# Block 1's output projection and the choice of four of its heads, moved ahead of the attention of blocks 2 and 3

## The chip, the cores and the metric

The kernel runs on one NeuronCore of a Trainium2 chip. Its five engines work side by side, each through a queue of its own in a fixed order: TensorE (PE, matrix products; PEld is its weight load), VectorE (DVE), ScalarE (ACT), GpSimd (POOL) and SyncE (SP, which here only issues transfers). What counts is the time of one execution on the device in microseconds. All arrays are float32.

## The reference

Two layers work on 512 tokens of width 1024. Only the first is touched by the change. It puts 16 learned tokens ahead, mixes by attention and a recurrence side by side, and then sends each token through a sum over experts chosen for it:

```python
proj = jnp.einsum('btd,dc->btc', a, w_in)
att = diff_attention(aq, ak, av, ...)      # 4 heads, two softmax maps each, blocks of 128 queries
rec = hgrn2(rq, rf, ri, rg, ...)           # gated recurrence, 4 heads
h = h + jnp.einsum('btc,cd->btd', jnp.concatenate([att, rec], -1), w_out)

def one_block(xb):                         # 128 tokens
    q = jnp.einsum('nd,dc->nc', xb, w_query).reshape(128, 8, 2, 128)
    s = jnp.einsum('nhpc,hpkc->nhpk', q, subkeys)
    sv, si = lax.top_k(s, 16)
    cand_s = sv[:, :, 0, :, None] + sv[:, :, 1, None, :]
    top_s, pos = lax.top_k(cand_s.reshape(128, 8, 256), 16)
    experts, gates = ..., softmax(top_s)   # 8 heads x 16 = 128 experts per token
    hid = gelu(einsum('nkd,nd->nk', u_table[experts], xb)) * gates
    return einsum('nk,nkd->nd', hid, v_table[experts])
```

Attention of a block of tokens needs the keys and values of itself and of the blocks ahead of it, and nothing of their attention's result. The output projection of a block needs that block's attention and recurrence alone; the choice of its experts needs its projection alone.

## The kernel before

The 512 tokens lie in four blocks of 128 (0 to 3), their running sum in `h`. Each block has 128 expert slots per token, and for each slot one **gather** (`gather`, L801) fetches for all 128 tokens the row of u and the row of v that token needs: 1 MB, by an indirect DMA that POOL issues, into one of six buffers `g`. DVE multiplies it with `xb` and sums (`dot`, L815); after each pair of slots ACT takes the gelu and DVE multiplies with the gate (L860); then the v half is added to `h` either by DVE (L834) or by PE through a diagonal matrix into `acc` (L829), as the table `PE_SLOTS` says. Only then is the buffer free for another gather. There are 512 gathers, and this text calls the 128 of block b **expert stage b**.

Everything else is woven among the gathers by hand. Each part of the program is a Python generator that yields after a step; `weave(main, side, rate)` takes `rate` steps of the side for every step of the main one, and one gather is one main step (130 in a stage). A scheduler then sets the last order of each engine's queue from that, and may shift instructions by some places.

- Stage 0 runs beside `until_first()`, that is `mixer([1, 2, 3])` up to its `yield "first"`, at 0.5 steps per gather; what is left of these steps when the gathers are used up follows without gathers.
- Stage 1 runs beside the rest of that mixer at 0.62, and then beside the selection of blocks 2 and 3 from scores kept aside (`slow[0]`, a fifth of a step each).
- Stage 2 runs beside what is left of that selection (`slow[1]`, a third of a step each), stage 3 beside the second layer for blocks 0 to 2, and block 3's second layer comes last.

In `mixer([1, 2, 3])` come projections and recurrence, then the attention of its three blocks (`attend`, seven steps for four heads and two more), `project_out` (L580 on PE with weights `wout`, L587 adds to `h`), then `choose_from` (the transposed rows `xT`, the row norm `rstd`) and `choose`: per head, queries by `wq` (L171), scores into the PSUM tile `psc` (L711), and for blocks 0 and 1 at once `select`, which finds the top 16 and computes the experts' numbers `idx` and the gates on DVE (L743 to L793). For blocks 2 and 3 the scores are kept. `ALONE` is the number of heads that block 1 chooses by itself, ahead of "first"; the others are chosen for blocks 1 to 3 in one product of 384 columns, and blocks 2 and 3 make up for the first `ALONE` heads afterwards in products of 256 columns. `need(b, g)` takes steps at once where a stage comes to the gathers of heads that aren't chosen yet; four heads give 64 gathers.

PSUM tiles of the tag "tr" are two: `psc`, the transposes `awT`, `tf`, `mxT` and the attention's result `aO` take turns in them.

Of the kernel before, what the change touches and what calls it, by code (L numbers as in the profile page):

```python
# [26 lines left out]
GROUPS = ((0, 1, 16), (1, 1, 8), (2, 2, 5), (4, 4, 3), (8, 8, 1))  # L27
NCAND = sum(n * w for _, n, w in GROUPS)
PE_SLOTS = {0: (8, 8, 16, 8), 1: (20, 24, 28, 26), 2: (16, 26, 10, 24), 3: (0, 0, 0, 0)}
RATE = {"1b": 0.5, "1c": 0.62, "2a": 0.62}  # L30
GBUFS = 6
RR = (2.8, 2.7)
FR = 2.0
PRE = 0
ANCHOR = 124
ALONE = 2
PACE = (5, 3)

CW = 256
# [3 lines left out]
def layer_pair_kernel(ctx: ExitStack, tc, a, dbg=None):  # L43
# [151 lines left out]
    def run(*gens):  # L195
        for g in gens:
            for _ in g:
                pass

    def chain(*gens):  # L200
        for g in gens:
            yield from g

    def weave(main, side, per, flush=True):

        due = 0.0
        for _ in main:
            yield
            due += per
            while due >= 1.0:  # L210
                due -= 1.0
                next(side, None)
        for _ in side if flush else ():
            yield
# [223 lines left out]
    def mixer(blocks, meta):  # L438

        nb = len(blocks)  # L440
# [34 lines left out]
        def cols(i):  # L475
            return slice(off + i * P, off + (i + 1) * P)
# [29 lines left out]
        def heads_to_features(po, tag, use):  # L506
            o = head_norm(po, tag)
            p4 = psum_t("mxT").rearrange("p (k t) -> p k t", k=4)
            for k in range(4):
                T.transpose(p4[:, k, :], o[:, k, :], ident)  # L510
            use(p4)
# [14 lines left out]
        def attend(i, b):  # L526
            dst = aq[:, :, cols(i)]
            o = t1.tile([P, 4, P], F32, tag="ao", name="ao")
            yield from attention_block(b, dst, lambda hd, po: V.tensor_copy(o[:, hd, :], po))
            yield  # L530
            heads_to_features(o.rearrange("p h v -> p (h v)"), "0",
                              lambda p4: V.tensor_scalar(dst, p4, subw, None, op0=ALU.mult))
            yield
# [55 lines left out]
        def project_out(part):  # L589
            for j in range(2):  # L590
                p = [(psum, psum, psum_c)[i]("wout") for i in range(len(part))]
                for half in (1, 0):
                    yield from out_half(j, half, part, p)
                out_add(j, part, p)
# [15 lines left out]
        def values(part):  # L610
            return tokens(2, lambda i: av[:, blocks[i], :], avm, part)

        if nb > 1:
            recs = [recurrent(i, blocks[i]) for i in range(nb)]
            yield from weave(chain(kq(None), values((0, 1))), chain(*recs), RR[0])
            yield from weave(feature(6, use_g, lo=off), attend(0, blocks[0]), RR[1])
            for i in range(1, nb):
                yield from attend(i, blocks[i])
            yield from project_out(list(range(nb)))
            choice = new_choice(blocks)  # L620
            yield from choose_from(choice, blocks[:1])
            yield from choose(choice, blocks[:1], range(ALONE))
            yield "first"
            yield from choose_from(choice, blocks[1:])
            yield from choose(choice, blocks, range(ALONE, 8))
            yield from choose(choice, blocks[1:], range(ALONE))
        else:
            rec = recurrent(0, blocks[0])
            for _ in feature(6, use_g, lo=off):
                yield  # L630
                next(rec)

            def also_rec(g):
                for _ in g:
                    yield
                    next(rec, None)

            yield from also_rec(kq((0,)))
            with after(state["load"]):
                for b in range(1, NB):  # L640
                    nc.sync.dma_start(h[:, b, :], x[b * P:(b + 1) * P, :])
                load_choice()
            yield from also_rec(values((0,)))
            wh = [None, None]
            att = attend_out(blocks[0], wh)
            yield from islice(att, 3)
            yield from also_rec(kq((1,)))
            yield from islice(att, 3)
            yield from also_rec(values((1,)))
            yield from rec  # L650
            for j in range(2):
                next(att)
                p = [psum("wout")]
                w = load_out(j, 1)
                with after(state["av"]):
                    for k in range(4):
                        T.matmul(p[0], qq[:, k, cols(0)], w[:, k, :], start=(k == 0), stop=(k == 3))
                out_add(j, [0], p)
                wh[j] = load_out(j, 0)
                yield  # L660
            yield from att
# [14 lines left out]
    def choose_from(choice, blocks):  # L676
        at, xT = choice
        for b in blocks:
            to_features(h[:, b, :], P, xT[:, :, at[b]], ffw)
            V.tensor_copy(rstd[:, b:b + 1], row_rstd(h[:, b, :], P, "", new_xn()))  # L680
            yield
# [154 lines left out]
    def experts(b):  # L836


        xb = make_xb(b, rstd[:, b:b + 1], t1.tile([P, D], F32, tag="xb", name="xb"))
        pe = by_pe(b)  # L840
        before = []
        for j in range(0, P + 2, 2):
            if j == P:
                for late in before:
                    add_row(b, *late)
                    yield
                return
            need(b, j // 32)
            d2 = t2.tile([P, 2], F32, tag="dots", bufs=4, name="dots")
            h2 = t2.tile([P, 2], F32, tag="hid", bufs=4, name="hid")  # L850
            now = []
            for i in range(2):
                g = gather(b, j + i)
                dot(b, j + i, xb, g, d2[:, i:i + 1])
                now.append((j + i, pe, g, h2[:, i:i + 1]))
                if before:
                    add_row(b, *before[i])
                yield
            S.activation(h2, d2, AF.Gelu)  # L859
            V.tensor_tensor(h2, h2, gate[b].rearrange("p h k -> p (h k)")[:, j:j + 2], op=ALU.mult)  # L860
            before = now
# [391 lines left out]
    def tally(name, g):  # L1253
        for v in g:
            steps[name] = steps.get(name, 0) + 1
            yield v
# [21 lines left out]
    slow = [paced(later, k) for k in PACE]  # L1278
# [8 lines left out]

    run(weave(experts(0), weave(tally("1b", until_first()), first, FR), RATE["1b"]))
    run(weave(experts(1), chain(tally("1c", rest), tally("1d", slow[0])), RATE["1c"], flush=False))
    run(rest)  # L1290
    load_second()
    run(weave(experts(2), tally("2z", slow[1]), RATE["1c"]))
    run(weave(experts(3), tally("2a", second([0, 1, 2])), RATE["2a"]))
    run(tally("2b", second_last(3)))
    if dbg is not None:
# [84 lines left out]
```

## Time and profile before

| | us |
|---|---|
| median of 3 runs (2003.7 to 2016.32) | 2010.13 |
| the profiled execution | 2004.79 |
| its span, first to last instruction | 2003.0 |

The profile shows one execution. A busy share is the part of a stretch in which an engine executed something; the DMA share is the mean of 16 transfer engines; PEclk is the clock that TensorE was granted, as a share of full speed. A view by windows adds these up over stretches of the span. A row of waits names an instruction, what released it, and the idle time ahead of it.

### The profile page before, as it was taken

The page shows a single profiled execution, that of the slowest core. Times are in us where ns is not written, and L with a number is a line of the kernel's source. Part 1 is how long each engine was busy: PE and PEld are TensorE (multiplying, and loading weights), DVE is VectorE, ACT ScalarE, POOL GpSimd, SP SyncE. Part 2 cuts the span into 40 slices and gives each one's busy share as a digit, 9 for nine tenths or more (in the row PEclk, how much of TensorE's full clock was granted, in tenths as well). Part 3 has the DMA queues.
Part 4 walks back from the last instruction along what each step waited for, and adds up shares of the span by engine and source line. Part 5 has one row for each costly group of instructions (what it writes and reads, how often), then busy time and mean ns, then how long its engine had stood idle before and what let it go on. Part 6 is the DMA issues. An engine that isn't in the chain of part 4 may idle for free.

```text
span 2003.0 us, 18269 instructions
## 1 busy us (share of the span) xinstructions
PE 1551.6 (77%) x5391; PEld 910.2 (45%) x5391; DVE 1628.4 (81%) x3944; ACT 609.1 (30%) x1255; POOL 684.0 (34%) x523
## 2 busy tenths in 40 slices
PE   8967898988788996667665575464699976888697
PEld 7844575753345563222222122121366543547475
DVE  3589999968987899997579956867967988788887
ACT  2213311236641232211121211011147642231574
POOL 0014333323420333444443445545533344443000
PEclk9988999998788997798896686679799978999799
DMA  9439998987884998999999999999998779999664
GB/s 391 181 145 368 385 357 330 346 305 280 322 301 149 394 364 320 341 354 377 402 404 345 360 384 394 416 395 402 388 391 320 288 249 355 404 385 359 251 232 178
DMA packets 94557, 666.57 MB, mean 333 GB/s; under 512 B 10789, under 2 KB 11230, under 8 KB 14330
## 3 DMA queue, kind: packets, MB, share of 16 engines
q0 software_dynamic: 73728, 536.90, 69.5%
q1 hardware_dynamic: 19394, 123.42, 15.9%
q10 hardware_dynamic: 1336, 5.08, 0.6%
q8 instruction: 43, 0.70, 0.1%
q14 instruction: 56, 0.46, 0.1%
HBM read 663.27 MB, written 2.10 MB: 332 GB/s over the span
## 4 chain that ended last, share of the span: by engine, by line
DVE 33%; PE 28%; issue 16%; DMA 10%; POOL 8%; ACT 5%; POOLq 0%; SPq 0%; ACTq 0%; DVEq 0%
PE win L171 15%; DVE g L815 11%; POOL g L801 8%; DMA g<-in_peer_uv_dram,idx 8%; DVE h L834 6%; PE wout L171 2%; DMA win<-in_w_in_dram 1%; DVE jt L764 1%; DVE ex L767 1%; DVE jt L766 1%; ACT L859 1%; PE acc L829 1%; PE pl L1129 1%; PE pl L1130 1%; DVE si L747 1%
## 5 line engine op out<-in xcount | busy, mean ns | idle before, releaser
L801 POOL DMA_INDIRECT g<-in_peer_uv_dram,idx x512 | 680.9, 1330 | 1148.4 <-DVE h L834 435.6
L815 DVE SCALAR_TENSOR_TENSOR g<-g,xb 128x1024 f32<-128x1024 f32 x512 | 622.8, 1217 | 147.2 <-DMA g<-in_peer_uv_dram,idx 144.4
L829 PE MATMUL acc<-g,dg 128*128 128x512 f32 x856 | 511.1, 744 | 272.9 <-ACT dg L826 272.8
L829 PEld LDWEIGHTS acc<-g,dg 128*128 128x128 f32 x856 | 187.8, 233 | 559.2 <-ACT dg L826 371.7
L171 PE MATMUL win<-aT,win 128*128 128x384 f32 (+2 forms) x1344 | 366.7, 428 | 26.9 <-DMA win<-in_w_in_dram 20.1
L834 DVE SCALAR_TENSOR_TENSOR h<-g,hid,h 128x1024 f32<-128x1024 f32 x298 | 381.0, 1279 | 3.6
L171 PEld LDWEIGHTS win<-aT,win 128*128 128x128 f32 x1344 | 228.6, 196 | 150.2 <-issue 28.9
L859 ACT ACTIVATE hid<-dots 128x2 f32<-128x2 f32 x256 | 52.1, 203 | 784.0 <-DVE g L815 777.8
L171 PE MATMUL wq<-xT,wq 128*128 128x128 f32 (+2 forms) x576 | 120.5, 361 | 2.1 <-DVE qq L490 2.1
L826 ACT ACTIVATE dg<-ident,hid 128x128 f32<-128x128 f32 x214 | 80.7, 398 | 87.3 <-DVE hid L860 72.3
L859 ACT ACT_TABLE_LOAD x79 | 101.4, 1283 | 11.0 <-DVE g L815 9.7
L171 PEld LDWEIGHTS wq<-xT,wq 128*128 128x128 f32 x576 | 86.2, 193 | 31.3 <-issue 5.9
L860 DVE TENSOR_TENSOR hid<-hid,gate 128x2 f32<-128x2 f32 x256 | 40.3, 158 | 60.7 <-ACT hid L859 60.4
L171 PE MATMUL win<-win,aT 128*128 128x256 f32 x384 | 86.9, 382 | 0.0
L1125 DVE TENSOR_TENSOR wlo<-wl,whi 128x1024 fp32r<-128x1024 f32 x60 | 72.3, 1218 | 11.9 <-PE pl L1130 5.0
L171 PEld LDWEIGHTS win<-win,aT 128*128 128x128 f32 x384 | 72.2, 191 | 11.9 <-issue 1.6
L1124 ACT CAST whi<-wl 128x1024 fp32r<-128x1024 f32 x60 | 60.1, 1047 | 29.8 <-DMA wl<-in_w_in_2t_dram 12.3
L379 PE MATMUL sc<-akT,aq 64*128 64x400 f32 (+3 forms) x80 | 32.9, 511 | 19.6 <-ACT ae L389 19.6
L149 PE MATMUL tf<-ident,xn 128*128 128x128 f32 x56 | 12.2, 382 | 40.3 <-DVE xn L973 22.4
L171 PE MATMUL wout<-wout,mg 128*128 128x256 f32 x192 | 41.9, 380 | 0.1
L815 DVE DVE_READ_ACCUMULATOR g<-g,xb 128x1 f32 x512 | 41.5, 81 | 0.0
L926 DVE TENSOR_TENSOR_SCAN rs<-kp,zero 128x128 f32<-128x128 f32 (+3 forms) x32 | 26.3, 823 | 18.2 <-ACT kp L924 18.1
(386 smaller groups left out, 1869.3 us busy)
## 6 DMA issues: line engine op xcount, KB each, us to landing
win<-in_w_in_dram SPq DMA_DIRECT2D x50, 1024.0 KB, 9.1
wq<-in_peer_w_query_dram SPq DMA_DIRECT2D x18, 1024.0 KB, 8.3
wl<-in_w_in_2t_dram SPq DMA_DIRECT2D x18, 1024.0 KB, 4.8
wout<-in_w_out_dram SPq DMA_DIRECT2D x12, 1024.0 KB, 8.5
g<-in_peer_uv_dram,idx POOLq DMA_INDIRECT x512, 8.6
wl<-in_w_in_2t_dram ACTq DMA_DIRECT2D x4, 1024.0 KB, 8.8
wl<-in_w_out_2t_dram SPq DMA_DIRECT2D x4, 1024.0 KB, 4.8
skT<-in_peer_subkeys_dram SPq DMA_DIRECT2D x9, 256.0 KB, 7.7
```

What stands on the lines that cost most here:

```text
L171: T.matmul(o, lhs(k), rhs(k), start=(k == 0), stop=(k == nk - 1))
L379: T.matmul(sc[:, 0:hi - lo], aq[rr, hd, :], akT[rr, hd, lo:hi], start=True, stop=(hi != L))
L801: G.indirect_dma_start(out=g, out_offset=None, in_=uv_tab, in_offset=bass.IndirectOffsetOnAxis(ap=idx[b][:, k:k + 1], axis=0))
L815: V.scalar_tensor_tensor(u, u, 1.0, xb, op0=ALU.mult, op1=ALU.mult, accum_out=o)
L826: S.activation(dg, ident, AF.Copy, scale=c)
L829: T.matmul(state["acc"][:, q], dg, g[:, D + j * 512:D + (j + 1) * 512], start=(k == pe[0]), stop=(k == pe[-1]))
L834: V.scalar_tensor_tensor(h[:, b, :], g[:, D:2 * D], c, h[:, b, :], op0=ALU.mult, op1=ALU.add)
L859: S.activation(h2, d2, AF.Gelu)
L860: V.tensor_tensor(h2, h2, gate[b].rearrange("p h k -> p (h k)")[:, j:j + 2], op=ALU.mult)
L926: V.tensor_tensor_scan(rs[:, 0:L][:, ::-1], kp[:, 0:L][:, ::-1], zero.to_broadcast([P, L]), 1.0, op0=ALU.mult, op1=ALU.add)
L1124: S.copy(hi, w[:, q, :])
L1125: V.tensor_tensor(lo, w[:, q, :], hi.bitcast(F32), op=ALU.subtract)
```

## The change

`project_out` is called once for block 1 alone (index 0 in the list of three) straight after its attention, and once for blocks 2 and 3 after theirs. Between the two, block 1's `choose_from` and the choice of its first heads take place, and now `ALONE` is 4 and not 2. The attention of blocks 2 and 3, their projection and the rest of the choice come after "first", and so into the steps that stage 1 is woven with. The side of stage 2 gets a rate of its own, 0.75 in place of 0.62.

```diff
-RATE = {"1b": 0.5, "1c": 0.62, "2a": 0.62}
+RATE = {"1b": 0.5, "1c": 0.62, "2z": 0.75, "2a": 0.62}
-ALONE = 2
+ALONE = 4
             yield from weave(feature(6, use_g, lo=off), attend(0, blocks[0]), RR[1])
-            for i in range(1, nb):
-                yield from attend(i, blocks[i])
-            yield from project_out(list(range(nb)))
+            yield from project_out([0])
             choice = new_choice(blocks)
             yield from choose_from(choice, blocks[:1])
             yield from choose(choice, blocks[:1], range(ALONE))
             yield "first"
+            for i in range(1, nb):
+                yield from attend(i, blocks[i])
+            yield from project_out(list(range(1, nb)))
             yield from choose_from(choice, blocks[1:])
             yield from choose(choice, blocks, range(ALONE, 8))
             yield from choose(choice, blocks[1:], range(ALONE))
-    run(weave(experts(2), tally("2z", slow[1]), RATE["1c"]))
+    run(weave(experts(2), tally("2z", slow[1]), RATE["2z"]))
```

Lines below the change have a number one higher in the kernel after it. Counted in yields, the mixer's part ahead of "first" had 76 steps (17 of projections, 14 and 4 woven ones, 18 of attention, 12 of projection, 1 and 10 of choice) and has 60 (17, 14, 4, then 4 of projection, 1 and 20 of choice), against 65 that 130 main steps at 0.5 take. The part after "first" had 38 and has 60 (18, 8, 2, 20, 12), against 80 at 0.62.

On PE, before, from the last expert products of stage 0 (`acc` with `dg`) over the projection (`wout`) to block 1's first choice (`wq` with 128 columns, `psc`) and to the first product of stage 1 (the last row):

```order
L829 MATMUL acc<-g,dg 128x512 x2
L580 MATMUL wout<-wout,aq 128x512 x8
L510 MATMUL mxT<-ident,hn 128x128 x4
L149 MATMUL tf<-ident,h 128x128 x4
L580 MATMUL wout<-wout,aq 128x512 x8
L149 MATMUL tf<-ident,h 128x128 x4
L171 MATMUL wq<-xT,wq 128x128 x16
...
L171 MATMUL wq<-xT,wq 128x384 x8
L711 MATMUL psc<-skT,qs 128x128 x3
L829 MATMUL acc<-g,dg 128x512 x2
```

And after the change, where the products of stage 0 (slots near 96 to 112 of its 128) stand among them, and the recurrence's half of the projection of blocks 2 and 3 and the transposes of block 2's attention follow the choice:

```order
L830 MATMUL acc<-g,dg 128x512 x2
L580 MATMUL wout<-wout,aq 128x512 x8
L830 MATMUL acc<-g,dg 128x512 x2
L149 MATMUL tf<-ident,h 128x128 x8
L171 MATMUL wq<-xT,wq 128x128 x16
L712 MATMUL psc<-skT,qs 128x128 x2
L830 MATMUL acc<-g,dg 128x512 x2
...
L171 MATMUL wq<-xT,wq 128x128 x13
L830 MATMUL acc<-g,dg 128x512 x2
L171 MATMUL wq<-xT,wq 128x128 x3
L712 MATMUL psc<-skT,qs 128x128 x2
L580 MATMUL wout<-wout,qq 128x512 x8
L409 MATMUL awT<-ident,ae 128x128 x3
```

The projection and the choice have moved from behind the last product of stage 0 to between its products.

On DVE, before, the end of block 1's second head (`jt`, `ex`, `idx`, the gates) stands right ahead of and behind the first dot of stage 1, with no dot for some 115 rows ahead of it:

```order
L791 TENSOR_REDUCE gz<-gate 128x2
L766 TENSOR_TENSOR jt<-jt,cx 128x432
L792 RECIPROCAL gz<-gz 128x2
L767 TENSOR_REDUCE ex<-jt 128x8
L793 TENSOR_TENSOR gate<-gate,gz 128x32
L764 TENSOR_TENSOR jt<-iota,pf 128x432
L766 TENSOR_TENSOR jt<-jt,cx 128x432
L815 SCALAR_TENSOR_TENSOR g,dots<-g,xb 128x1024
L767 TENSOR_REDUCE ex<-jt 128x8
L768 CAST idx<-ex 128x16
```

After the change the last dot of stage 0 (the second row), the `xb` of stage 1 and its first dot (the eighth row) are these, with the attention of block 3 (`amx`, `az`, `ao`) between them:

```order
L835 SCALAR_TENSOR_TENSOR h<-g,hid,h 128x1024
L816 SCALAR_TENSOR_TENSOR g,dots<-g,xb 128x1024
L391 TENSOR_TENSOR az<-az 128x1
L835 SCALAR_TENSOR_TENSOR h<-g,hid,h 128x1024
L666 SCALAR_TENSOR_TENSOR xb<-h,rstd,ffnw 128x1024
L395 RECIPROCAL az<-az 128x1
L861 TENSOR_TENSOR hid<-hid,gate 128x2
L816 SCALAR_TENSOR_TENSOR g,dots<-g,xb 128x1024
L835 SCALAR_TENSOR_TENSOR h<-g,hid,h 128x1024
L587 TENSOR_TENSOR h<-wout,h 128x512
```

The choice of the first heads is no longer between the two stages; five rows lie between the two dots.

## Rows read from the trace of the kernel before

**Rows 1.** The page: busy time of the engines; DMA in 40 slices.
```profile
PE 1551.6 (77%) x5391; PEld 910.2 (45%) x5391; DVE 1628.4 (81%) x3944; ACT 609.1 (30%) x1255; POOL 684.0 (34%) x523
...
DMA  9439998987884998999999999999998779999664
```
**Rows 2.** Windows of stages: us, PE, PEld, DVE, ACT, POOL busy (x), PEclk, DMA, GB/s.
```profile
132.96:592.90 459.94, 383.48 (x1450) 236.45 (x1451) 404.68 (x1000) 168.24 (x354) 163.06 (x128) 0.88 0.89 332
592.90:644.90 52.00, 42.70 (x174) 26.02 (x173) 37.51 (x130) 7.86 (x19) 0.05 (x2) 0.87 0.46 178
644.90:1032.80 387.90, 295.12 (x739) 140.30 (x737) 331.63 (x1088) 84.59 (x220) 158.65 (x130) 0.89 0.94 367
1032.80:1382.70 349.90, 203.33 (x316) 73.01 (x316) 269.62 (x594) 55.60 (x157) 167.84 (x129) 0.75 0.98 386
```
**Rows 3.** Timeline of POOL: the last gather of stage 0, the first of stage 1.
```profile
591.96 0.94 POOL L801 DMA_INDIRECT g<-in_peer_uv_dram,idx  x1 [0.30 <-issue]
644.86 0.94 POOL L801 DMA_INDIRECT g<-in_peer_uv_dram,idx  x1 [51.95 <-DVE idx L768]
```
**Rows 4.** Waits of DVE in that pause, 592.9 to 644.9.
```profile
DVE h L587 <- PE wout L580: 5.2, 3, 2.7
...
DVE sx L743 <- PE psc L711: 2.4, 1, 2.4
```
**Rows 5.** Windows of nine stretches, 16 dots each, columns as in rows 2.
```profile
438.10:498.10 60.00, 49.73 (x147) 23.42 (x146) 47.77 (x114) 38.47 (x83) 18.46 (x17) 0.86 0.82 299
498.10:549.50 51.40, 38.16 (x111) 19.51 (x112) 46.17 (x109) 31.97 (x68) 20.98 (x17) 0.72 0.87 323
549.50:605.00 55.50, 43.47 (x132) 21.90 (x131) 44.67 (x92) 23.29 (x53) 15.49 (x13) 0.81 0.83 305
605.00:708.00 103.00, 97.78 (x355) 58.46 (x356) 83.92 (x300) 20.69 (x48) 22.34 (x20) 0.95 0.71 274
708.00:766.90 58.90, 54.96 (x211) 35.63 (x209) 57.63 (x214) 18.72 (x46) 19.51 (x16) 1.00 0.93 364
766.90:819.40 52.50, 36.28 (x56) 13.42 (x56) 51.84 (x201) 13.77 (x30) 21.02 (x15) 0.74 0.82 303
819.40:867.30 47.90, 29.75 (x56) 12.01 (x56) 47.78 (x170) 9.94 (x25) 21.34 (x19) 0.82 0.94 356
867.30:915.00 47.70, 31.81 (x56) 12.21 (x56) 47.39 (x190) 9.48 (x25) 21.02 (x17) 0.86 0.93 353
915.00:957.60 42.60, 30.62 (x56) 12.02 (x56) 26.00 (x58) 6.59 (x22) 17.55 (x17) 0.88 0.98 391
```
**Rows 6.** DVE by lines, 766.9 to 819.4 (times done | busy us, mean ns | idle before).
```profile
L815 DVE SCALAR_TENSOR_TENSOR g<-g,xb 128x1024 f32<-128x1024 f32 x16 | 19.4, 1210 | 0.0
L834 DVE SCALAR_TENSOR_TENSOR h<-g,hid,h 128x1024 f32<-128x1024 f32 x4 | 5.1, 1273 | 0.0
...
L767 DVE TENSOR_REDUCE ex<-jt 128x8 f32<-128x432 f32 x8 | 4.7, 591 | 0.0
...
L860 DVE TENSOR_TENSOR hid<-hid,gate 128x2 f32<-128x2 f32 x8 | 1.2, 153 | 0.0
```
**Rows 7.** DVE by lines, 549.5 to 605, attention of block 3.
```profile
L382 DVE TENSOR_REDUCE amx<-sc 128x1 f32<-128x400 f32 (+1 forms) x8 | 3.3, 425 | 1.2 <-PE sc L379 1.2
L399 DVE SCALAR_TENSOR_TENSOR ae<-ae,az 128x528 f32<-128x528 f32 x3 | 2.3, 760 | 0.0
L398 DVE TENSOR_SCALAR ae<-ae,az,nlam 128x528 f32<-128x528 f32 x3 | 1.6, 549 | 0.0
```
**Rows 8.** Waits of PE, 438 to 592.9.
```profile
PE sc L379 <- ACT ae L389: 19.6, 10, 4.1
```
**Rows 9.** Timeline of PE in the pause: `wq` of one head's half, the score.
```profile
629.00 0.39 PE L711 MATMUL psc<-skT,qs 128*128 128x128 f32 x2
629.22 1.95 PE L171 MATMUL wq<-xT,wq 128*128 128x128 f32 x16
```
**Rows 10.** Timeline of DVE in the pause: the last read of that first score.
```profile
633.43 0.28 DVE L745 MATCH_REPLACE8 tkt<-sx,psc 128x128 f32<-128x128 f32 x1
```

## The prediction

> **What bounds the kernel now.** I read the page first. DVE is busy for 81% of the span of 2003.0 us, PE for 77%, and the transfers stand at nine or ten tenths in most slices [rows 1]. No engine is the bound everywhere, so I went stage by stage. The slices of the transfers have one hole in the middle, at the thirteenth slice (600 to 650 us), and the windows by stage show it as a pause: 52 us between the stages 0 and 1, with the DMA share at 0.46 against 0.89 and 0.94 on its sides [rows 2]. The timeline of POOL gives the reason: the last gather of stage 0 is issued at 591.96, the next at 644.86 after 51.95 us of waiting for `idx` on DVE [rows 3], because block 1's experts aren't chosen until then. Stage 2 on the other hand is held by transfers (share 0.98, DVE busy 269.62 of 349.90 us) [rows 2].
>
> The pause is not empty, though. In its 52 us PE is busy for 42.70 and DVE for 37.51 [rows 2], with projection, choice and the last five dots; DVE's idle 14.5 us are mostly waits, the longest of them for the projection (5.2) and the scores (2.4) [rows 4]. This work has to be done anyhow. So the pause is no measure of the gain. I looked instead at nine stretches of 16 dots around it, S1 to S9, from slot 80 of stage 0 to slot 95 of stage 1, which take 519.5 us with 453.2 us of DVE work [rows 5]. Two patterns are to be seen there. Where the gathers run beside attention (S1 to S3), DVE is idle for 12.2, 5.2 and 10.8 us, and ACT's exponential and PE's scores take turns in waiting: PE waits 19.6 us for ACT's reading of the scores before it can write new ones [rows 8]. Where they run beside choice (S5 to S8), DVE is full: 57.63 of 58.90, 51.84 of 52.50 and so on. S4, which holds the pause, has 19.1 us idle. In S9 the transfers bound (0.98) and DVE has 16.6 us to spare.
>
> **The change part by part.** *No DVE work is added or removed*: the same heads are selected for the same blocks, the same rows projected. What can be gained is idle DVE time, 66.3 us in the nine stretches (519.5 less 453.2), less what the transfers force in S9. I price the pieces from rows. A chosen head: in S6 DVE's 51.84 us less 19.4 of dots, 5.1 of additions and 1.2 for eight small `hid` products leave 26.1 us for four heads (L767 comes twice per head, x8) [rows 5, 6], 6.5; S8 gives the same way (47.39 less 19.4, 2.5, 1.2 for 3.5 heads) 6.9. I take 6.8. A head of attention in block 3: 3.3, 2.3 and 1.6 us for the big operations of three heads [rows 7], 2.4 each, about 3 with the small ones.
>
> Then the order of the changed kernel says what stands among which dots. S1 gains only a norm (+3 us). S2 (slots 96 to 111 of stage 0) gains 3.5 heads of choice (23.8), a block's transposes and norm (3), a projection add (0.7), and gives up one head of attention and smaller things (-6): 46.2 becomes 67.5. S3 gains half a head and part of block 3's attention: 44.7 becomes 50.5. S4 gives up about five heads of choice (-34) and two adds, and takes one head of attention: 83.9 becomes 47.5. S5 gives up one head: 57.6 becomes 50. S6 to S9 take +4.8, +1.2, +0.8 and +7.2, since selection is pushed back by the attention now in front: 56.6, 49, 48.2, 33.2. Together 453, as it must be.
>
> Now the time of each stretch. S1 is as it was with a little more: 61. S2 is bounded by DVE as S5 to S8 are; they run at 1.00 to 1.02 of DVE's busy time, S2's attention today at 1.11, and I take 1.04: 70. S3 stays an attention stretch, between 1.11 and today's 1.24: 58. S4 loses the pause; DVE needs 47.5, the transfers about 42 (S9), PE an estimated 55 of its 97.8 (by the count of its rows, since block 1's choice and half of the projection now come earlier and the joint products spread into S5 and S6): 53. S5 is led by the joint product for four heads on PE: 54. S6 57.5, S7 49.5, S8 48.5 at DVE's pace, S9 43 at that of the transfers. Sum 494.5 against 519.5: **-25 us**.
>
> Most of this is S4 with S2 and S3 read together: 209.9 us become 181. The idle time that goes is 13 to 14 us in the pause, 8 us in the attention stretches (where choice rows stand ready while an exponential is awaited) and 7 us in S9, less some 3 us in S5 to S8, which were full and now have PE or transposes ahead of them.
>
> *Transfers.* Block 1 projects alone and so `wout` is loaded twice (+4 MB), two more heads are computed twice (`wq` +2 MB), one more `skT` (0.25 MB): +6.25 MB on SP's queue. At the 391 GB/s of S9 that is 16.8 us if nothing covered it. Loads and gathers share the engines; in S1 to S4, where the loads fall, the share is 0.71 to 0.87 over 270 us, which leaves some 50 us free [rows 5]. I take 0, and 17 as the other end. SP's queue has only such loads in it, each waiting for a buffer, so nothing else is held up.
>
> *PE.* Two heads with 128 and 256 columns in place of 384 are the same number of columns; 16 products with 128 take 1.95 us [rows 9], and three times that for 384 would be 5.9. I take 0. The choice moves from S4 (clock 0.95) into S2 (0.72) [rows 5]: four heads are 128 such products, 15.6 us at full clock and some 21.6 at 0.72, beside 38.2 less about 7 of attention that leaves: 53 of 70 us. DVE covers it; without that cover it would be 6 us.
>
> *Stages 2 and 3.* 0.75 for stage 2 covers the heads that stage 1 leaves over. From slot 96 of stage 1 on DVE's order has the same content to within two rows in a stretch; 0, give or take 3 us for shifts by the scheduler.
>
> The profiled execution took 2004.79 us; 2004.8 - 25 = 1979.8. The median of the runs lies 5.3 above that execution, so the forecast as a median is **1985 us**. About 1% (20 us) is what a measurement of this kernel can tell from no change.
>
> *A rule weighed.* POOL's time per gather is 1.40 us in S6 (21.02 for 15), where DVE is full, 1.22 in S5, and 1.03 in S9 (17.55 for 17), where DVE is busy for 61% [rows 5]. The Trainium skill, page "SBUF — State Buffer", section "SBUF: two separate sides", says that DVE in certain modes locks GpSimd out of a shared port, so that descriptors of GpSimd's transfers aren't written until the DVE instruction ends. That speaks against a change that puts gathers beside choice. The trace agrees in sign; but POOL is idle for 60% of such a stretch (51.4 less 21.0 in S2), since it waits for buffers, so in my sum the dearer issue costs nothing.
>
> **The rivals.**
>
> *Nothing much is gained (about 2003 us).* The pause goes, but the idle time comes back as waits between attention and choice, both of which now have in-order queues through PE, ACT and DVE. If S1 to S5 (266 us of DVE work) run at 1.18 of it, they take 314; with S6 to S9's 198.5 that is 512.5, -7 us. For: S1 and S3 run at 1.26 and 1.24 today. Against: S2, also attention, runs at 1.11, and DVE's order puts rows of choice between those of attention.
>
> *Slower (about 2024 us).* One mechanism: the two "tr" tiles. A score holds one of them from its product at 629.0 to DVE's last read at 633.7, 4.7 us, on an empty engine [rows 9, 10]. In S2 and S3 such tiles now alternate with those of attention: awT, aO and one more per head, 26 for the two blocks. PE is in order, so the wait of a transpose for a tile also holds the `acc` products behind it, and these free the gathers' buffers. If each of the 26 waits 1.5 us, that is 39 us, less the 25: +14. It decides from about 1 us per tile. For: 4.7 us held and only two tiles. Against: the scheduler puts a score's four products and its DVE reads close together, and in stage 0's start, where choice runs beside the recurrence, DVE is full, not idle.
>
> *DVE never waits (about 1955 us).* If choice fills every gap, S1 to S8 take DVE's 420 us and S9 42.6: 462.6, -57; with the 2% of S5, some -48. For: S5 to S8 do so. Against: S1 has nearly the same content as today.
>
> *The issue on POOL decides (1997 us).* If gathers in S2 and S3 were held by 0.37 us each (1.40 less 1.03) and nothing hid it, 32 of them cost 12 us, and the gain is 13. For: the two rows; against: POOL's idle time. By the page's rule this would be larger still, up to a whole DVE instruction per issue.
>
> That the change doesn't do what it says (the choice is placed early, but scheduled late) I leave out as a case of its own: the order of DVE shows block 1's selection between slots 101 and 120.
>
> **How the numbers follow.** Forecast 0.52, with its own range 1967 to 2000 (S3 and S4 at 1.05 to 1.24, the loads' 17 us partly seen); no gain 0.21; slower 0.11; DVE full 0.12; POOL 0.04. Faster by over 1% means under 1990: 0.42 of the forecast and all of "DVE full", 0.54. Slower by over 1% (above 2030) is the worse half of its rival and a little of the loads, 0.08. The rest, 0.38, is within 1%. The range leaves out the farther half of "DVE full" and the farther part of "slower": 1962 to 2020.
>
> **What would show it.** In the profile after: no wait of POOL over 15 us between the stages; S1 to S9 taking about 495 us with the same 453 us of DVE; S2 the longest stretch but one with DVE over 93% busy; S4 near 53; queue q1 6.5 MB heavier; stage 2 at 350 us still. I am wrong if PE's wait for ACT's exponential (19.6 us) grows well beyond 30, if transposes wait for PSUM tiles in S2 and S3, or if the time that the pause gives back turns up in stages 1 or 2 as a DMA share near 1.

## The result and the profile after

The changed kernel takes 1981.4 us as a median, the kernel before 2007.01 in the runs beside it; the ratio is 0.9874 with a 95% interval of 0.9844 to 0.9904. One disturbed run is left out of the ratio. The profiled executions took 1978.65 us (span 1976.9) and 2004.79 us (span 2003.0), 26.1 us apart. The forecast was 1985 us, and 25 us between the executions. So the total came out as forecast; the next rows show that most of it came from another place.

The page of the changed kernel, the line of PE and the other engines, the slices of the transfers, and SP's queue:

```profile
PE 1547.2 (78%) x5455; PEld 915.8 (46%) x5455; DVE 1626.8 (82%) x3944; ACT 603.7 (31%) x1254; POOL 678.3 (34%) x523
...
DMA  9539998988968999899999999999999878999664
...
q1 hardware_dynamic: 20402, 129.97, 16.9%
```

The hole in the slices [rows 1] is smaller and earlier: a 6 in the twelfth slice in place of a 4 in the thirteenth. The engines do the same work (DVE 1626.8 us against 1628.4). The same line of the kernel before gives SP's queue 123.42 MB, so 6.55 MB were added (the prediction's 6.25 counted in units of 1024 x 1024 bytes):

```profile
q1 hardware_dynamic: 19394, 123.42, 15.9%
```

The timeline of POOL in the changed kernel, at the last gather of stage 0 and the first of stage 1, answers [rows 3]:

```profile
620.37 1.30 POOL L802 DMA_INDIRECT g<-in_peer_uv_dram,idx  x1 [0.30 <-issue]
622.33 1.22 POOL L802 DMA_INDIRECT g<-in_peer_uv_dram,idx  x1 [0.66 <-DVE h L835]
```

The wait of 51.95 us is now one of 0.66. The pause is gone. The windows of the changed kernel, cut at the same dots, answer [rows 5] with the nine stretches S1 to S9 and [rows 2] with stage 2; the last two are stage 3 and what follows its last dot:

```profile
436.00:500.70 64.70, 52.90 (x156) 25.26 (x155) 51.12 (x128) 38.22 (x84) 17.87 (x16) 0.82 0.81 309
500.70:577.30 76.60, 58.97 (x262) 37.98 (x260) 67.44 (x223) 20.58 (x53) 19.48 (x17) 0.86 0.85 335
577.30:630.70 53.40, 38.11 (x98) 19.85 (x99) 49.11 (x129) 24.22 (x57) 19.49 (x15) 0.65 0.78 278
630.70:683.60 52.90, 46.75 (x141) 23.66 (x140) 44.10 (x99) 14.29 (x38) 22.14 (x17) 0.94 0.95 377
683.60:741.90 58.30, 58.30 (x200) 34.33 (x199) 51.08 (x166) 13.60 (x34) 18.34 (x16) 1.00 0.95 368
741.90:804.70 62.80, 56.53 (x218) 37.58 (x216) 59.96 (x234) 18.84 (x47) 21.54 (x18) 0.95 0.97 376
804.70:854.90 50.20, 34.23 (x54) 12.94 (x54) 48.87 (x188) 14.92 (x32) 20.17 (x15) 0.76 0.80 293
854.90:904.80 49.90, 32.17 (x64) 13.14 (x64) 48.15 (x189) 9.48 (x25) 17.94 (x18) 0.86 0.90 346
904.80:949.00 44.20, 29.09 (x56) 11.15 (x56) 32.49 (x94) 6.71 (x22) 19.27 (x17) 0.92 0.96 376
1031.90:1376.80 344.90, 201.04 (x316) 70.76 (x314) 269.46 (x596) 55.65 (x156) 170.25 (x129) 0.76 0.98 389
1376.80:1834.50 457.70, 388.70 (x1365) 245.03 (x1366) 390.15 (x678) 174.98 (x284) 184.45 (x126) 0.90 0.91 358
1834.50:1976.90 142.40, 118.49 (x533) 88.29 (x531) 117.78 (x180) 91.40 (x122) 0.00 (x0) 0.93 0.61 222
```

The last three windows of the kernel before, at the same dots:

```profile
1039.40:1387.90 348.50, 201.35 (x316) 72.04 (x314) 269.85 (x596) 55.30 (x156) 168.79 (x130) 0.76 0.98 386
1387.90:1859.00 471.10, 386.72 (x1368) 244.53 (x1368) 392.82 (x695) 169.95 (x282) 188.44 (x125) 0.90 0.90 349
1859.00:2003.00 144.00, 120.46 (x528) 89.44 (x528) 115.50 (x162) 90.29 (x120) 0.00 (x0) 0.89 0.58 212
```

S1 to S9 take 513.0 us in place of 519.5, a gain of 6.5 where 25 were forecast. Stage 3, for which 0 was forecast, gives 13.4. The rest is 2.1 before S1, 3.6 in stage 2, 1.6 at the end, less 1.1 in the last two stretches of stage 1. DVE is busy in stage 3 for as long as before (390.15 and 392.82), so it waits less. Its longest waits there, of the kernel before and then of the changed one (us, times, longest):

```profile
DVE hid L860 <- ACT hid L859: 24.0, 35, 4.0
DVE g L815 <- DMA g<-in_peer_uv_dram,idx: 18.1, 14, 3.7
DVE rs L926 <- ACT kp L924: 15.2, 11, 3.4
DVE h L1057 <- PE wout L171: 7.9, 5, 3.0
...
DVE ya L1009 <- PE py L1007: 3.4, 3, 1.6
```

```profile
DVE hid L861 <- ACT hid L860: 19.7, 33, 2.8
DVE g L816 <- DMA g<-in_peer_uv_dram,idx: 13.6, 14, 2.5
DVE rs L927 <- ACT kp L925: 13.3, 9, 2.7
DVE ya L1010 <- PE py L1008: 6.0, 3, 2.6
DVE h L1058 <- PE wout L171: 5.5, 5, 1.9
```

The first four of before add up to 65.2 us, the same four after to 52.1; the wait for `py` grows by 2.6. The net of 10.5 is most of stage 3's 13.4. The edit doesn't touch stage 3. But the order of DVE's rows differs there: only some two thirds of them stand in the same sequence as before, and PE's and ACT's differ too, while the work is the same: the scheduler, which orders the whole program, gave it another order. Whether that order made the 13 us, or one execution merely ran better than another, was the first question for the experiments. The second was where the forecast gain in S1 to S9 had gone.

### The profile page after: what moved, and what is told of

It reads as the page before. It is cut to its first block, busy times and chain, and to the rows that moved or that the text cites. A ratio compares the mean times of both kernels' runs of the same rounds, so it can differ in the third digit from the quotient of the medians.

```text
span 1976.9 us, 18409 instructions
## 1 busy us (share of the span) xinstructions
PE 1547.2 (78%) x5455; PEld 915.8 (46%) x5455; DVE 1626.8 (82%) x3944; ACT 603.7 (31%) x1254; POOL 678.3 (34%) x523
## 4 chain that ended last, share of the span: by engine, by line
PE 35%; DVE 30%; issue 14%; DMA 9%; POOL 8%; ACT 4%; POOLq 0%; SPq 0%; ACTq 0%; DVEq 0%
PE win L171 15%; DVE g L816 10%; POOL g L802 8%; DMA g<-in_peer_uv_dram,idx 7%; DVE h L835 6%; PE acc L830 3%; PE wq L171 3%; DMA win<-in_w_in_dram 1%; PE wout L171 1%; PE wout L580 1%; PE pu L171 1%; DVE jt L765 1%; DVE jt L767 1%; DVE ex L768 1%; PE pl L1131 1%
## 5 line engine op out<-in xcount | busy, mean ns | idle before, releaser
L830 PE MATMUL acc<-g,dg 128*128 128x512 f32 x856 | 505.4, 736 | 257.1 <-ACT dg L827 250.7
L171 PEld LDWEIGHTS win<-aT,win 128*128 128x128 f32 x1344 | 229.3, 196 | 148.6 <-issue 31.6
L860 ACT ACTIVATE hid<-dots 128x2 f32<-128x2 f32 x256 | 52.1, 204 | 766.5 <-DVE g L816 762.2
L827 ACT ACTIVATE dg<-ident,hid 128x128 f32<-128x128 f32 x214 | 81.1, 398 | 103.0 <-DVE hid L861 77.9
L171 PEld LDWEIGHTS wq<-xT,wq 128*128 128x128 f32 x640 | 93.7, 193 | 29.4 <-issue 7.2
L1126 DVE TENSOR_TENSOR wlo<-wl,whi 128x1024 fp32r<-128x1024 f32 x60 | 72.2, 1218 | 8.3 <-PE pl L1131 2.1
L379 PE MATMUL sc<-akT,aq 64*128 64x400 f32 (+3 forms) x80 | 33.9, 528 | 24.9 <-ACT ae L389 24.9
L1129 PE MATMUL pl<-whi,xs 128*128 128x512 f32 x88 | 36.4, 416 | 5.7 <-ACT xs L1075 5.1
```

What stands on the lines that cost most here:

```text
L171: T.matmul(o, lhs(k), rhs(k), start=(k == 0), stop=(k == nk - 1))
L379: T.matmul(sc[:, 0:hi - lo], aq[rr, hd, :], akT[rr, hd, lo:hi], start=True, stop=(hi != L))
L827: S.activation(dg, ident, AF.Copy, scale=c)
L830: T.matmul(state["acc"][:, q], dg, g[:, D + j * 512:D + (j + 1) * 512], start=(k == pe[0]), stop=(k == pe[-1]))
L1126: V.tensor_tensor(lo, w[:, q, :], hi.bitcast(F32), op=ALU.subtract)
L1129: T.matmul(p, lhs[0][:, k, :], hi[:, i, :], start=(k == 0), stop=False)
```

## The experiments

Medians and ratios are of runs beside the kernel before on the same chip: e1 to e4 on one chip, e5 to e8 on a second, e9 to e12 on a third. The other columns are of one profiled execution each. S1 to S9 are cut at the same dots in each, as is stage 3 (from the last dot of stage 2 to its own last dot); "end" is what follows.

| kernel | S1–S9 | stage 3 | end | median | ratio (95%) |
|---|---|---|---|---|---|
| before | 519.5 | 471.1 | 144.0 | 2007.0 | |
| after | 513.0 | 457.7 | 142.4 | 1981.4 | 0.9874 (0.9844–0.9904) |
| e1 rate alone | 521.3 | 471.4 | 143.8 | 2008.6 | 0.9990 (0.9965–1.0015) |
| e2 no rate | 511.9 | 459.1 | 148.6 | 1990.1 | 0.9885 (0.9831–0.9939) |
| e3 move, two heads | 504.2 | 466.1 | 140.3 | 1988.6 | 0.9893 (0.9843–0.9943) |
| e4 old place, four heads | 518.7 | 467.6 | 140.3 | 2006.4 | 0.9994 (0.9968–1.0021) |
| e5 old place, rate 0.55 | 507.5 | 450.3 | 149.4 | 1983.6 | 0.9872 (0.9830–0.9914) |
| e6 new place, rate 0.55 | 504.8 | 452.1 | 150.1 | 1976.9 | 0.9842 (0.9798–0.9887) |
| e7 projection alone | 521.5 | 459.2 | 146.5 | 2003.1 | 0.9961 (0.9931–0.9992) |
| e8 old place, six heads | 526.7 | 458.3 | 146.1 | 2005.4 | 0.9976 (0.9952–1.0001) |
| e9 fewer additions on PE | 505.4 | 451.7 | 141.5 | 1977.0 | 0.9871 (0.9833–0.9909) |
| e10 joint loads twice | 522.7 | 461.9 | 146.2 | 2002.8 | 0.9977 (0.9954–1.0000) |
| e11 two heads, rate 0.55 | 500.8 | 461.3 | 143.3 | 1975.4 | 0.9857 (0.9820–0.9893) |
| e12 two heads, FR 2.4 | 492.6 | 452.2 | 149.4 | 1980.2 | 0.9873 (0.9835–0.9911) |

**The parts of the change.** First the new rate of stage 2 alone, and the change without it. These two kernels have row for row the order of the kernel before and of the changed kernel, so they also are repeats of both:

```
e1:  before, with  RATE["2z"] = 0.75 and weave(..., RATE["2z"]) for stage 2
e2:  after, with   "2z": 0.75  ->  "2z": 0.62
```

> The kernel before with stage 2's rate at 0.75 alone. The order of all five engines is row for row that of the kernel before, so this is also a second profile of that program. Both theories expect the ratio 1.00. They differ on stage 3 (first dot to last dot, 471.1 us in the profile before and 457.7 in the one after). Theory ORDER (the other order of DVE's queue in stage 3 of the changed kernel makes those 13 us): 471 within 4 us here. Theory CHANCE (transfers run a little faster or slower from one execution to the next): anywhere from 455 to 475. Nine stretches S1 to S9: 519 within 4 us for both.

> The changed kernel with stage 2's rate back at 0.62. The order of all engines is row for row that of the changed kernel, so this is its second profile. Ratio to the kernel before 0.987 for both theories. ORDER: stage 3 takes 458 within 4 us and S1 to S9 513 within 4 us. CHANCE: stage 3 anywhere from 455 to 475, so that the gain of the profile shown would be partly luck and the nine stretches would have to hold more than 6.5 us of the true gain.

The rate does nothing, and both numbers repeat: 521.3 and 511.9 us in S1 to S9, 471.4 and 459.1 in stage 3. With the repeats the gain in S1 to S9 is 8.0 us (520.4 to 512.45) and in stage 3 12.9 (471.25 to 458.4). Stage 3's gain isn't chance. Not all of it reaches the total, though: what follows stage 3 takes 148.6 us in e2 and 142.4 in the changed kernel, so stage 3 and the end together gain 15.0 us in the first pair of profiles and 7.5 in the repeats.

Then the move with two heads ahead, and four heads chosen alone at the old place:

```
e3:  after, with   ALONE = 4  ->  ALONE = 2
e4:  before, with  ALONE = 2  ->  ALONE = 4
```

> The move alone, with two heads chosen ahead and not four. If the pause is what cost, the gain of S1 to S9 is here in full or more, since less choice is crowded into S2 (two heads there in place of three and a half): 505 to 513 us for S1 to S9, POOL without a wait over 15 us between the stages. If four heads early are needed (gathers of stage 1 wait for the choice of heads 2 and 3, which now comes behind two blocks of attention), a new pause of 10 to 30 us appears at slot 32 of stage 1 and S1 to S9 take 515 to 530. Stage 3's order is a third one here, between 455 and 475 us; total 1978 to 2000.

> Four heads chosen ahead without the move: attention and projection of all three blocks still come first. If the place of the choice behind attention makes the pause, the pause stays at some 50 us and S1 to S9 take 519 to 530, with up to 6 us more for loads and the split products; ratio 1.00 to 1.01. If the number of heads matters by itself, S1 to S9 shorten by 3 us or more. Stage 3's order is nearly that of the run with the move and two heads, so its time there should be within 4 us of that run's under ORDER.

The number of heads at the old place changes nothing (0.9994), and POOL still waits 51.41 us between the stages in e4. With two heads ahead S1 to S9 take 504.2 us, 8 less than with four. S2 alone is 10 us shorter (66.3 us against 76.6 in the changed kernel and 76.5 in e2), with less choice in it (60.8 us of DVE work in place of 67.4), and this kernel loads 2.36 MB less than the changed one (q1 127.61 MB). Stage 3 takes 466.1 and 467.6 in this pair, which has nearly one order there. So what tells e3 from e4 lies in S1 to S9: 14.5 us (518.7 and 504.2), more than the 8.0 of the change, though the number of heads differs as well.

**Order or place.** Two pairs were chosen such that PE, DVE and ACT have the same order, row for row, from about the end of S9 on, while what stands ahead of it differs. In e5 block 1's choice stands at the old place and in e6 at the new one. In e8 it stands at the old place too, and in e7 only block 1's projection has moved ahead: its choice stays behind the attention of blocks 2 and 3.

```
e5:  before, with  RATE["1b"] = 0.5  ->  0.55
e6:  after, with   RATE["1b"] = 0.5  ->  0.55
e7:  after, with   ALONE = 4  ->  ALONE = 0
e8:  before, with  ALONE = 2  ->  ALONE = 6
```

> The kernel before, with the rate of the side work beside stage 0 raised from 0.50 to 0.55 and nothing else. Block 1's projection and choice stay behind the attention of blocks 2 and 3, so the pause stays. From the middle of stage 2 on, the order on PE, DVE and ACT is row for row that of the next kernel, and much nearer to the changed kernel's (0.83 of DVE's rows of stage 3 in the same sequence, against 0.65 for the kernel before). ORDER (stage 3 follows from the order that the scheduler happens to give it): stage 3 takes 456 to 464 us in place of 471, S1 to S9 about 520 as before, the median some 10 us under the kernel before although the pause stands. CHANCE or MOVE (stage 3 is shorter by chance, or because of what the move itself did): stage 3 stays at 471, the median within 5 us of the kernel before.

> The changed kernel with the same rate of 0.55. Its stages 2 and 3 have the order of the kernel beside it (the last 773 rows of PE, 1216 of DVE and 629 of ACT are the same), so that the difference of the two is the place of block 1's projection and choice alone. ORDER: stage 3 within 3 us of the kernel beside it, and a difference in the sums S1 to S9 of 6 to 12 us, as between the kernels before and after (6.5) and their repeats (9.4); the medians differ by that. The forecast of 25 us for the place alone would show as 495 against 520.

> The changed kernel with none of block 1's heads ahead: only its output projection and the transposes of its normalized rows stand ahead of the attention of blocks 2 and 3, the choice of all eight heads behind it. If the pause is what the choice costs, it stays: a wait of POOL of 35 to 50 us between the stages, S4 near 90 us, S1 to S9 515 to 521. If the projection was what mattered, S1 to S9 fall to about 510. Stage 3 by ORDER: 0.87 of DVE's rows stand in the sequence of the kernel before, so 466 to 472.

> The kernel before with six of block 1's heads chosen alone in place of two, behind the attention as before. From the middle of stage 2 on its order is that of the kernel beside it (the last 775 rows of PE, 1217 of DVE, 626 of ACT). ORDER: stage 3 within 3 us of the kernel beside it. The pause grows, since more heads stand ahead of the joint choice and nothing else moves: S4 105 to 115, S1 to S9 519 to 530.

Windows of e5, S1 to S9 and stage 3, and the same of e6:

```profile
435.30:942.80 507.50, 403.88 (x1163) 202.52 (x1163) 451.07 (x1427) 171.42 (x393) 179.36 (x145) 0.87 0.86 329
1371.00:1821.30 450.30, 379.84 (x1330) 237.53 (x1331) 388.89 (x671) 173.04 (x280) 181.40 (x126) 0.90 0.92 362
```

```profile
438.70:943.50 504.80, 405.47 (x1220) 211.20 (x1220) 448.96 (x1429) 163.58 (x387) 176.12 (x145) 0.86 0.89 344
1373.10:1825.20 452.10, 380.16 (x1331) 237.31 (x1332) 388.88 (x671) 172.59 (x280) 182.91 (x126) 0.89 0.92 361
```

Stage 3 follows its order and not the place: 450.3 and 452.1 in one pair, 459.2 and 458.3 in the other, 471.1 and 471.4 for before and e1 (e9, below, is an exception by 6 to 7 us). The sizes that were expected for e5 and e7 (456 to 464, 466 to 472) were missed by 6 and 7 us, since they were read from how many rows stand in the same sequence: a likeness of 0.83 or 0.87 to a known order gave no time. DVE's waits for ACT's `hid` in stage 3 of e5 are down to 15.8 us:

```profile
DVE hid L860 <- ACT hid L859: 15.8, 31, 2.1
```

e5 is the telling one. Nothing is moved in it, and POOL still waits 41.83 us between the stages:

```profile
626.33 0.94 POOL L801 DMA_INDIRECT g<-in_peer_uv_dram,idx  x1 [41.83 <-DVE top L777]
```

It is as fast as the changed kernel (0.9872 and 0.9874). Stage 3 is 20.8 us shorter than in the kernel before, and the end of the program gives a part back (149.4 us against 144.0). But S1 to S9 are shorter too, 507.5 us where some 520 were expected: with the pause still in them they take less than the 513.0 of the changed kernel. Most of that is in S4 (90.7 us for 103.0) and S1 (53.2 for 60.0); why the higher rate brings it was not taken apart. With equal orders behind it, the move is worth 2.7 us in S1 to S9 at this rate, where 6 to 12 were expected, and the medians (1983.6 and 1976.9) are not told apart by their intervals. So the move was worth 2.7, 8.0 and 14.5 us in S1 to S9, with different work around it. In e7 POOL waits 34.71 us between the stages: the projection without the choice doesn't remove the pause, as expected, and S1 to S9 stay at 521.5. In e8 the pause did not grow as expected (51.32 us, S4 100.2 for 105 to 115).

**Where S1 to S9 lost their gain.** In S5 of the changed kernel PE is busy for all of 58.30 us, and the transfers stand at 0.95 to 0.97 in S4 to S6. e9 takes work from PE, e10 gives more to the transfers:

```
e9:   add_row:       + if b == 1 and k in pe and 16 <= k < 48: return
e10:  feature_proj:    w = load_w(src, c0 + j * CW, name)
                     + if name == "wq" and n == 3 * P:
                     +     nc.sync.dma_start(w, src[(c0 + j * CW) // CW])
```

> The changed kernel without the additions that PE makes for the experts 16 to 47 of block 1 (their products with a diagonal, ACT's making of it, nothing else): these experts are gathered and dotted, but not added, so this part of the output is left out. S5 and S6 are the stretches where PE was full or near it (58.4 of 58.4 and 56.5 of 62.7 us), transfers at 0.95 and 0.97, DVE at 51.1 and 59.9. From slot 97 of stage 2's order on, everything is row for row as in the changed kernel. PE (TensorE sets the pace of S5): S5 falls to 53 to 55 us, S6 to 61, the two together from 121 to about 115. TRANSFERS (the loads that were costed at nothing set it): S5 and S6 together stay at 119 to 122. Stage 3 at 457 to 460 by ORDER in either case.

> The changed kernel with each strip of the query weights for the joint choice of blocks 1 to 3 loaded twice into its tile (4 MB more, from S4 to S6; the same work on the engines). TRANSFERS: 4 MB at the 377 GB/s of S4 are 11 us, so S4 to S6 grow from 174 to 182 or more. PE or DVE at the bound: they stay within 3 us of 174. Stage 3's order is another one again (0.77 of DVE's rows as in the kernel before), so by ORDER its time is not 458 but nearer to 465 to 470, and the median is no measure of the loads.

Windows of e9, S5 and S6; then of e10, S4 to S6:

```profile
681.66:741.13 59.47, 58.12 (x237) 40.11 (x235) 53.36 (x187) 12.99 (x33) 20.34 (x18) 1.00 1.01 415
741.13:802.02 60.89, 27.91 (x100) 19.27 (x100) 58.28 (x237) 15.56 (x32) 19.14 (x17) 0.66 0.88 340
```

```profile
631.28:692.07 60.79, 52.14 (x166) 27.23 (x165) 45.83 (x113) 15.26 (x40) 21.60 (x18) 0.94 0.98 386
692.07:757.05 64.98, 64.85 (x242) 41.88 (x241) 59.23 (x209) 18.33 (x43) 17.92 (x16) 1.00 0.93 365
757.05:820.02 62.97, 49.16 (x148) 26.93 (x146) 57.47 (x228) 17.32 (x41) 19.17 (x18) 0.86 0.82 310
```

With 22 additions (88 of PE's rows) less, PE does 86.0 us of work in S5 and S6 in place of 114.8, and the two take 120.4 us in place of 121.1. So a quarter less of PE's work gained nothing in the two; joint products moved up into S5, so that PE is full there in e9 too (58.12 of 59.47 us), and the transfers went to 1.01. S1 to S9 as a whole took 505.4 us, 7 less than in the changed kernel and its repeat, in small parts outside S5 and S6 and with 3 us less of DVE work; that was not taken apart. e10 has 4.2 MB more (q1 134.17 MB) and the same DVE work in S1 to S9 (451.33 us); the sum grows by 10.2 us to 522.7, S4 to S6 from 174.0 to 188.7. DVE's waits for gathers in S1 to S9 grow from 22.6 us in the changed kernel to 31.5:

```profile
DVE g L818 <- DMA g<-in_peer_uv_dram,idx: 31.5, 26, 3.7
```

The part of the growth in S4 to S6 that goes beyond 10 us is DVE work that came earlier (162.5 us in the three against 155.1) and is missing in S9 (41.3 us). At S4's 377 GB/s 4.2 MB are 11 us: in these stretches an added load cost nearly its full time. In e10 each strip is also ready later by its second load, and how much of the 10 us is that wait wasn't separated. e10's stage 3 (461.9) lies 3 us below its expectation. e9's stage 3 (451.7) lies 5 us below its own, though its order is that of the changed kernel; that is the largest spread seen within one order, and the two were profiled in different sets of runs. That leaves 450 and 458 us hardly told apart as orders, while 458 and 471 are.

**A faster version.** Two heads ahead (less to load) with the rates that gave a good stage 3:

```
e11:  after, with  ALONE = 2 and RATE["1b"] = 0.55
e12:  after, with  ALONE = 2 and FR = 2.4
```

> A version to beat both: the move with two heads (ALONE = 2) and the rate beside stage 0 at 0.55. With two heads ahead S1 to S9 took 504 us, with the higher rate the other two kernels lost 6 to 13 us there, so 492 to 500. Stage 3's order is 0.96 that of the kernels with 459 us, so by ORDER 457 to 462. Sum: some 1970 us as a median. If stage 3's time has nothing to do with its order, 471 and 1983.

> Another version to beat both: the move with two heads and 2.4 in place of 2.0 steps of block 0's choice beside one step of the mixer. Stage 3's order is 0.97 that of the kernels with 451 us: by ORDER 449 to 455. S1 to S9 about 504 as with two heads, since the choice of block 0 lies ahead of it. Some 1970 us as a median; if stage 3's time doesn't follow its order, 1985.

Both expectations for stage 3 held: 461.3 and 452.2, with orders 0.96 and 0.97 alike to known ones. The medians of some 1970 us did not come (1975.4 and 1980.2). e12's S1 to S9 can't be compared with the others, since its S1 begins some 14 us later (452.5 against 438): choice moved ahead of it. e11's S1 to S9 took 500.8 us, just above the 492 to 500 expected. It has the lowest median, but its ratio of 0.9857 overlaps with that of the changed kernel, so no version is shown to be faster.

## Why the prediction was right, and where it was not

The time was right, and of the mechanism the direction. But the term for S1 to S9 was three times too large (25 us for 8.0), and stage 3, taken at nothing, gave 13.

- **The pause and DVE's work: right. The idle time that goes: not.** POOL waits 0.66 us between the stages. DVE's work in the nine stretches sums to 452.3 us, forecast 453, and stands within 3.5 us of the forecast in each (S2 67.4 for 67.5, S4 44.1 for 47.5, S6 60.0 for 56.6). But DVE is idle for 60.7 us in them. Before it was 66.3, and the forecast's sum has 41.5. S2, which was to have DVE busy for over 93%, has 88%.
- **"Transfers: I take 0, and 17 as the other end": not settled.** With 16.8 us for the loads (6.55 MB at 391 GB/s) the forecast's own sum gives 511.3 us, measured 513.0 and 511.9. The same sum gives 505.2 us for e3 (4.19 MB added; 504.2 measured) and 522.0 for e10 (10.75 MB; 522.7). That speaks for the loads as the cause. Against it are e6 and e11, which lie 6.5 and 4.4 us under that line at the other rate, and the place of the loads. These are the lines of SP's queue in S1 and S2 and in S4 to S6 of the changed kernel, and in S3 and in S4 to S6 of the kernel before, which has none in S1 and S2 (packets, MB):

```profile
q1 hardware_dynamic: 1584, 9.96, 17.3%
q1 hardware_dynamic: 1872, 12.06, 17.4%
```

```profile
q1 hardware_dynamic: 285, 2.08, 9.0%
q1 hardware_dynamic: 2163, 13.39, 16.0%
```

  So what was added runs in S1 and S2, where the lists of waits of DVE and PE have none for a transfer, and where room is left (shares 0.81 and 0.85). S4 to S6 carry less than before. DVE's waits for gathers in all nine stretches did not grow, in the kernel before and then in the changed one:

```profile
DVE g L815 <- DMA g<-in_peer_uv_dram,idx: 23.0, 17, 3.4
```

```profile
DVE g L816 <- DMA g<-in_peer_uv_dram,idx: 22.6, 20, 3.3
```

  That the added loads cost 17 us is thus not shown. What the forecast did miss is S4 to S6. Their loads are no new ones, but before, these stretches took 214.4 us with the pause in them; now the loads run beside gathers in 174.0 us, at shares of 0.95 to 0.97. That is the share near 1 in stage 1 that the prediction named as a sign against itself. Gathers and loads there are 64.3 MB, 164.5 us at 391 GB/s, and 164.5 us is what the forecast gave the three stretches: nothing was left for any wait. e10 shows that 4.2 MB more in them cost 10 us.
- **S2: mis-sized by 6.6 us (76.6 for 70).** DVE's work was as forecast, but S2 took 1.14 times as long as that work, not 1.04. DVE's waits there are for PE and ACT (`wout` 2.6, `aO` 2.5, `ae` 2.1, `hid` 1.1). "PE. I take 0" left out how PE's order would be filled. A timeline of the changed kernel, PE and then ACT:

```profile
543.30 8.35 PE L580 MATMUL wout<-wout,qq 128*128 128x512 f32 x16
551.48 0.49 PE L409 MATMUL awT<-ident,ae 128*128 128x128 f32 x3
```

```profile
552.12 0.48 ACT L412 COPY awt<-awT 128x384 f32<-128x384 f32 x1 [9.46 <-PE awT L411]
```

  The first column half of the second projection, of blocks 2 and 3, stands here in one run ahead of attention's transposes and of the experts' additions. ACT waits 9.46 us for a transpose and POOL 18.71 us for a buffer that those additions free (18.67 in e2). That is the one wait over 15 us that is left around the two stages, and it isn't between them. But the run alone doesn't explain S2's length: in e6 the products of a score stand in the middle of it, ACT waits 1.79 us and POOL 12.55, and S2 takes 76.6 us again (PE, then the window):

```profile
534.40 3.60 PE L580 MATMUL wout<-wout,qq 128*128 128x512 f32 x8
537.83 0.38 PE L712 MATMUL psc<-skT,qs 128*128 128x128 f32 x2
538.05 3.60 PE L580 MATMUL wout<-wout,qq 128*128 128x512 f32 x8
```

```profile
496.30:572.90 76.60, 58.54 (x267) 37.60 (x265) 68.71 (x232) 24.45 (x61) 18.38 (x17) 0.86 0.84 333
```

  What makes S2 long stays open.
- **S5 and S6: 121.1 us for 111.5.** Of these 9.6 us, 4.4 are DVE work that comes later than forecast (111.0 us for 106.6; S4 has 3.4 less), the rest is idle time. "Led by the joint product on PE" isn't borne out for the two together: with a quarter less of PE's work they take as long in e9. S3 took 53.4 for 58, the other way. S1 and S7 to S9 add 7.0.
- **"Stages 2 and 3: 0, give or take 3": wrong by 13 us in stage 3, and it saved the number.** "Shifts by the scheduler" was the right cause with a wrong size. The runs show 450 to 471 us for the same work in different orders, and differences of at most 1.8 us between two kernels of one order (7 with e9).
- **The rivals.** "Nothing much is gained" put S1 to S9 at 512.5 us, and 513.0 was measured: in these stretches its sum came true, and not the forecast's. It laid the time into S1 to S5, as waits between attention and choice; they take 305.9 us, about halfway between its 314 and the forecast's 296. PE's wait for the exponential is 24.9 us from S1 to S3, which isn't the growth beyond 30 that would have spoken for it [rows 8]. The view is of PE's waits in the changed kernel, 436 to 630.7:

```profile
PE sc L379 <- ACT ae L389: 24.9, 11, 4.6
```

  "tr" tiles held nobody in the changed kernel: PE's longer waits in S2 are for operands that ACT makes (`dg` 4.8, `qs` 3.5, `awt` 3.0) and for ACT's reading of the scores (`sc` 4.0). "The issue on POOL": POOL took 1.15 us per gather in S2 (19.48 for 17) and stood idle for most of it, waiting for buffers; nothing hung on it. The rule that was weighed there (the Trainium skill, page "SBUF — State Buffer", section "SBUF: two separate sides": DVE in certain modes keeps GpSimd from writing a transfer's descriptors) shows no clear sign in these windows. POOL took 1.34 us per gather in S7, where DVE is busy for 97%, but 1.00 in S8, with 96%, and 1.13 in S9, with 74%. The prediction read a sign from three rows of before, but a fourth speaks against it: 1.12 in S7 (21.34 for 19), where DVE is full [rows 5].

That the total fell on the forecast is thus luck: S1 to S9 gave 18.5 us less than forecast, and the rest of the program 19.6 more than the nothing it was given, 13.4 of it in stage 3.

## What to carry to other kernels

Where a scheduler orders the whole program, an edit also reorders stages it doesn't touch, and that can be worth as much as the edit: here 21 us between the slowest and the fastest order of the same stage 3, and a change of one rate by 0.05 that moves no code gained as much as the move, two thirds of it in stage 3. So compare the stages behind the edit first, and judge the edit between kernels whose later order is the same. Free transfer time inside a pause goes with the pause: cost the loads that had run in it at the share that the stretch will have, not at the one it has. And look up in which stretch an added load really runs before it is blamed.

## What was not expected of the hardware

- In S5 of e9 the transfers moved 415 GB/s at a share of 1.01 (the view counts a transfer wholly where it starts, so a share can pass 1), above the 391 GB/s of S9 that the prediction took as the pace when full [rows 5]. The kernel before itself moved 409 GB/s at 1.00 right behind S9, from 957.6 to 1039.4.
- One stretch in which PE is full and DVE waits for no transfer repeats to a tenth of a microsecond: the third 16 dots of stage 3 take 74.3 us in the changed kernel, e2, e5, e6, e9 and e12 alike (in the changed kernel PE is busy for all 74.30 us at a granted clock of 1.00), and 72.2 in the kernel before, e1, e7, e8 and e11.
